# Backward SSD states: products and decays by head on ScalarE, the sum on VectorE

## The chip, the cores and the metric

The kernel runs on one core of a Trainium2 chip. The metric is the time of one execution on the device in microseconds; of several runs the median counts. A core has five engines, each with an instruction queue of its own: TensorE (PE, matmuls; PEld its weight loads), VectorE (DVE), ScalarE (ACT), GpSimd (POOL) and SyncE (SP), whose queue issues nearly all of this kernel's DMAs. Tiles lie in SBUF; matmuls write to PSUM.

## The reference, cut to what matters

The program is a backbone block of two layers over 1280 tokens, 256 of context and 1024 latent ones. Each layer projects the tokens, mixes them with two recurrences (an SSD group and an S5 group, both in both directions), and ends in a gated feed-forward net. The SSD scan works in chunks of 128 tokens; this is the part that the change touches, called once per direction:

```python
cum = jnp.cumsum(dt * a.reshape(SSD_GROUPS, SSD_HPG), axis=2)
xdt = xh * dt[..., None]
to_end = jnp.exp(cum[:, :, -1:] - cum)
states = jnp.einsum('bcqgn,bcqgep->bcgepn', bm, xdt * to_end[..., None])
chunk_decay = jnp.exp(cum[:, :, -1])

def step(h, inp):
    s, d = inp
    return h * d[..., None, None] + s, h
```

So a chunk gives a state from its values `xh`, weighted per token and head, and the running state is decayed by one number per head before the chunk's own is added. There are 8 heads of 64 channels; the running state of one direction is a tile of 128 by 512.

## The kernel before, in words

A layer goes through stages. After the projections for the S5 inputs comes a stretch in which VectorE runs the S5 scan: `s5_scan` makes one step after the other, four small tensor operations each (lines 545, 548, 549 and 550, tiles `sc` and `X`), and `s5_pairs` ends it with 96 operations on line 517. The whole scan is written into the program before the stage that follows.

In that stage `layer` (lines 1662 on) lets two things run together. `proj_z` makes the z projections: matmuls of 256 to 384 columns on lines 751 to 753 into four PSUM tiles `mm`, a ScalarE activation into `zb`, and a store. The generator `ssd_state` advances two steps with each piece of them and treats ten chunks in the order 1, 0, 9, 8, ..., 2. For a chunk it loads `xb` (six blocks of 128 by 128), transposes them on TensorE into two PSUM tiles, copies these to `xs` on ScalarE (lines 1196 and 1200), multiplies the values with `te` on GpSimd into `xe` (line 1168, in `ssd_xe`), and one step later stores `xs`, makes the state with two matmuls (`ssd_sum`) and hands it to `ssd_chain`. For the backward direction (`d` is 1, tile `hhb`) `ssd_chain` copies the state from PSUM to `hs` (line 1222, ScalarE), decays the running state (line 1223, GpSimd) and adds the two (line 1224, GpSimd). The first backward state is a plain copy (line 1219). Chunk 2 needs no backward state, so there are nine products and eight decays and sums in each layer. The forward direction (`hhf`), which also goes through `ssd_chain`, runs in the next stage, decayed on GpSimd and added on VectorE (lines 1226 and 1227).

The PSUM tiles `ps` of the transposes, the states and some small work share four buffers; in layer 0 the product of the conditioning weights (`adaw`) holds one of them for long. `xe` and `hs` share three buffers with the tag `yt`.

When all z projections are made and `ssd_state` is at its end, `s5_save` writes the scan's result to DRAM, eight stores `xh<-X`. SP's queue then goes on with loads for the next stage, among them `bto`, `xso` (values of a chunk), `cumrow` (decays) and later `xh`. Within a queue the order is fixed when the program is built: a scheduler places the instructions, and the helper class `Queue` only adds an order between a few of them. An instruction of a queue waits until those ahead of it have been issued.

Of the kernel before, what the change touches and what calls it, by code (L numbers as in the profile page):

```python
# [9 lines left out]
F32 = mybir.dt.float32  # L10
F32R = mybir.dt.float32r
I32 = mybir.dt.int32
AF = mybir.ActivationFunctionType
OP = mybir.AluOpType
AX = mybir.AxisListType

P = 128
# [81 lines left out]
class Kern:  # L99
# [1079 lines left out]
    def ssd_state(self, cs, S, xbc, dr, pool):  # L1179

        nc = self.nc
        XB, XT, XE = {}, {}, {}
        hb = None
        for t in range(len(cs) + 3):
            if t < len(cs):
                c = cs[t]
                XB[t] = pool.tile([P, 6, P], F32, name="xb", bufs=2)
                self.sp.dma_start(XB[t], xbc[4:10, :, c * P:(c + 1) * P].rearrange("m p t -> p m t"))
            t -= 1
            if 0 <= t < len(cs):  # L1190
                c, xb = cs[t], XB.pop(t)
                xt = XT[t] = pool.tile([P, 768], F32, name="xs", bufs=3)
                ps = self.psum()
                for i in range(4):
                    self.pe.transpose(ps[:, i * P:(i + 1) * P], xb[:, i], self.ident)
                nc.scalar.copy(xt[:, :512], ps)
                ps = self.psum()
                for i in range(2):
                    self.pe.transpose(ps[:, i * P:(i + 1) * P], xb[:, 4 + i], self.ident)
                nc.scalar.copy(xt[:, 512:], ps[:, :2 * P])  # L1200
                if c != 2:
                    XE[t] = self.ssd_xe(xt[:, :512], c, 1, S, pool)
            t -= 1
            if 0 <= t < len(cs):
                c, xt = cs[t], XT.pop(t)
                self.sp.dma_start(dr["xt"][c], xt)
                if c != 2:
                    hb = self.ssd_chain(self.ssd_sum(xt[:, 512:], XE.pop(t)), hb, c, 1, S, pool, "hb")
                    self.defer(1, lambda c=c, hb=hb: self.sp.dma_start(dr["hb"][c], hb))
            yield  # L1210

    def ssd_chain(self, cur, prev, c, d, S, pool, tag):

        nc, v, g = self.nc, self.nc.vector, self.nc.gpsimd
        h = pool.tile([P, 512], F32, name="h" + tag, tag=tag, bufs=2 if d else 3)
        v8 = lambda a: a.rearrange("p (h e) -> p h e", h=8)
        et = S["etot"][:, c, d].unsqueeze(2).to_broadcast([P, 8, 64])
        if prev is None:
            nc.scalar.copy(h, cur)
        elif d:  # L1220
            t = pool.tile([P, 512], F32, name="hs", tag="yt", bufs=self.ytb)
            nc.scalar.copy(t, cur)
            g.tensor_tensor(v8(h), v8(prev), et, op=OP.mult)
            g.tensor_tensor(h, h, t, op=OP.add)
        else:
            g.tensor_tensor(v8(h), v8(prev), et, op=OP.mult)
            v.tensor_tensor(h, cur, h, op=OP.add)
        return h
# [890 lines left out]
```

## Time and profile before

| what | value |
|---|---|
| median of three runs | 3443.62 us (3442.58 to 3463.33) |
| profiled execution | 3467.04 us, its span 3465.3 us |
| busy TensorE, VectorE, ScalarE, GpSimd | 3088.8, 2060.4, 1454.7, 1104.2 us |
| GpSimd product `xe` of the backward states | 9 per layer, 1.04 us each |
| GpSimd decay and sum | 8 per layer, 1.04 and 1.28 us each |
| the stage in layer 0, in layer 1 | from 434.4 us and from 2264.0 us of the span |

Positions are microseconds from the span's start. A line like L1224 is line 1224 of the kernel; L55 stands for the helper that records TensorE's and SP's instructions, so there the names of the tiles tell the place. In a name pair the tile before the arrow is written and those behind it are read. The busy time of an engine says nothing of its worth for the end; for that one has to see what waits where.

### The profile page before, as it was taken

Reading aid. Unit: us, or ns where it says so; the run is one execution under the profiler, and the core shown is the slowest. Engines: PE = TensorE matmul, PEld = TensorE weight load, DVE = VectorE, ACT = ScalarE, POOL = GpSimd, SP = SyncE. Lnnn points to the kernel's source line nnn. Section 1 sums busy time; section 2 is a strip of 40 time slices with the busy share of each in tenths; the row PEclk is TensorE's granted clock in tenths of the full one; section 3 lists DMA queues with packets and bytes.
Section 4 is the critical chain, followed back from the end, with each engine's and each line's share of the span. In section 5 each row is a group of like instructions: output and inputs, shape, how many; then the busy total and the mean of one; then the engine's idle time right before and its main releaser. Section 6 shows DMA issues by size and latency. Waiting matters only on the chain. (4 is left out here: it accounts for less than half of the span.)

```text
span 3465.3 us, 48617 instructions
## 1 busy us (share of the span) xinstructions
PE 3088.8 (89%) x18067; PEld 2673.7 (77%) x18067; DVE 2060.4 (59%) x3789; ACT 1454.7 (42%) x2610; POOL 1104.2 (32%) x847
## 2 busy tenths in 40 slices
PE   7689796898899999899999879775898999999998
PEld 4578674678879999889999769774576777877876
DVE  4875982456644444653344887993556655566555
ACT  4324522544543434543334443522545544454443
POOL 3651451213312323322222341451233333233230
PEclk8899897889999999999999889886889999999999
DMA  7345378525472222663322426268524533354332
GB/s 234 114 139 178 116 239 212 169 76 159 145 223 77 69 78 75 205 209 115 111 92 75 134 87 202 67 215 193 147 84 145 176 115 93 100 161 121 93 96 72
DMA packets 587281, 468.80 MB, mean 135 GB/s; under 512 B 59076, under 2 KB 506190, under 8 KB 587045
## 3 DMA queue, kind: packets, MB, share of 16 engines
q1 hardware_dynamic: 586565, 465.53, 44.5%
q8 instruction: 142, 2.33, 0.3%
q14 instruction: 94, 0.77, 0.1%
q0 software_dynamic: 480, 0.17, 0.0%
HBM read 355.99 MB, written 109.61 MB: 134 GB/s over the span
## 5 line engine op out<-in xcount | busy, mean ns | idle before, releaser
L860 POOL TENSOR_TENSOR ws<-rw,ws 128x512 fp32r<-128x512 f32 x352 | 483.9, 1377 | 1033.4 <-ACT ws L859 764.0
L752 PE MATMUL mm<-unit,ws 128*128 128x320 f32 (+3 forms) x2112 | 714.8, 338 | 3.4 <-POOL unit L901 3.4
L751 PE MATMUL mm<-unit,ws 128*128 128x320 f32 (+3 forms) x2112 | 716.5, 339 | 0.2 <-ACT unit L900 0.2
L753 PE MATMUL mm<-unit,ws 128*128 128x320 f32 (+3 forms) x2112 | 713.5, 338 | 0.0
L1439 DVE SCALAR_TENSOR_TENSOR fc<-fr,fcols,fc 128x255 f32<-128x255 f32 (+2 forms) x220 | 207.3, 958 | 492.7 <-ACT fc L1432 492.7
L751 PE MATMUL mm<-unit,whi 128*128 128x320 f32 (+3 forms) x1264 | 429.1, 341 | 38.0 <-ACT unit L900 23.4
L753 PE MATMUL mm<-unit,wlo 128*128 128x320 f32 (+3 forms) x1264 | 421.1, 334 | 31.4 <-POOL ub L996 19.0
L751 PEld LDWEIGHTS mm<-unit,ws 128*128 128x128 f32 x2112 | 398.0, 188 | 46.6 <-issue 10.1
L752 PEld LDWEIGHTS mm<-unit,ws 128*128 128x128 f32 x2112 | 398.0, 188 | 36.1 <-POOL unit L901 4.6
L753 PEld LDWEIGHTS mm<-unit,ws 128*128 128x128 f32 x2112 | 397.9, 188 | 34.7 <-issue 3.4
L752 PE MATMUL mm<-unit,whi 128*128 128x320 f32 (+3 forms) x1264 | 421.8, 334 | 2.6 <-POOL unit L901 1.6
L742 POOL TENSOR_TENSOR wlo<-raw,whi 128x1024 fp32r<-128x1024 f32 (+1 forms) x86 | 230.6, 2682 | 361.9 <-ACT whi L741 328.2
L751 PEld LDWEIGHTS mm<-unit,whi 128*128 128x128 f32 x1264 | 253.0, 201 | 74.7 <-ACT unit L900 25.4
L859 ACT CAST ws<-rw 128x512 fp32r<-128x512 f32 x352 | 218.4, 621 | 206.0 <-PE mm L753 116.8
L753 PEld LDWEIGHTS mm<-unit,wlo 128*128 128x128 f32 x1264 | 253.6, 201 | 47.3 <-POOL ub L996 19.2
L1519 DVE TENSOR_TENSOR acc<-mm,acc 128x256 f32<-128x256 f32 (+2 forms) x336 | 185.0, 554 | 171.2 <-PE mm L753 170.3
L752 PEld LDWEIGHTS mm<-unit,whi 128*128 128x128 f32 x1264 | 254.1, 201 | 15.3 <-issue 6.0
L751 PE MATMUL mm<-g,wd 128*128 128x320 f32 (+3 forms) x708 | 243.7, 345 | 10.8 <-ACT wd L859 6.8
L753 PE MATMUL mm<-g,wd 128*128 128x320 f32 (+3 forms) x708 | 241.5, 343 | 6.5 <-DVE wd L860 6.3
L752 PE MATMUL mm<-g,wd 128*128 128x320 f32 (+3 forms) x708 | 242.0, 342 | 0.0
L895 ACT COPY fr<-mm 128x320 f32<-128x320 f32 (+3 forms) x264 | 125.2, 476 | 195.1 <-PE mm L753 194.8
L1441 DVE SCALAR_TENSOR_TENSOR fc<-fr,fcols,fc 128x255 f32<-128x255 f32 (+2 forms) x220 | 176.0, 815 | 3.5
(390 smaller groups left out, 5761.5 us busy)
## 6 DMA issues: line engine op xcount, KB each, us to landing
rw<-in_ffn_w_up_dram SPq DMA_DIRECT2D x352, 256.0 KB
adaw<-in_w_ada_dram SPq DMA_DIRECT2D x80, 512.0 KB
raw<-in_ffn_w_down_dram SPq DMA_DIRECT2D x96, 384.0 KB
raw<-in_w_in_dram SPq DMA_DIRECT2D x40, 512.0 KB
raw<-in_w_out_dram SPq DMA_DIRECT2D x32, 512.0 KB
unit<-in_w_ada_dram SPq DMA_DIRECT2D x32, 256.0 KB
wt<-ws SPq DMA_DIRECT2D x32, 256.0 KB
ct<-w SPq DMA_DIRECT2D x64, 128.0 KB
```

The lines of the kernel that those rows point to most:

```text
L742: (eng or nc.vector).tensor_tensor(lo[:, :m], raw[:, :m], hi[:, :m].bitcast(F32), op=OP.subtract)
L751: mm(ps, whi[:, k], ahi[:, sl], start=first and k == 0, stop=False)
L752: mm(ps, whi[:, k], alo[:, sl], start=False, stop=False)
L753: i = mm(ps, wlo[:, k], ahi[:, sl], start=False, stop=last and k == len(a) - 1)
L859: self.nc.scalar.copy(hi, x)
L860: eng.tensor_tensor(lo, x, hi.bitcast(F32), op=OP.subtract)
L895: self.nc.scalar.copy(t[:, o:o + c], x)
L1439: v.scalar_tensor_tensor(cr[:, :, 1:], rr[:, :, :w - 1], f[0][:, ft:ft + 1], cr[:, :, 1:], op0=OP.mult, op1=OP.add)
L1441: v.scalar_tensor_tensor(cr[:, :, :w - 1], rr[:, :, 1:], f[2][:, ft:ft + 1], cr[:, :, :w - 1], op0=OP.mult, op1=OP.add)
L1519: v.tensor_tensor(acc[m][:, o:o + c], ps, acc[m][:, o:o + c], op=OP.add)
```

## The change

In `ssd_state` the product with `te` is made on ScalarE straight from the PSUM tile of the transposes, one activation per head of 128 by 64. In `ssd_chain` the backward decay is made on ScalarE too, again eight activations with a scale of one number per partition, and the state is added by one VectorE operation that reads it from PSUM; the copy to `hs` is gone, and GpSimd has no part in this stage's states. The forward direction is as it was.

```diff
@@ ssd_state
-                ps = self.psum()
+                px = self.psum()
                 for i in range(4):
-                    self.pe.transpose(ps[:, i * P:(i + 1) * P], xb[:, i], self.ident)
-                nc.scalar.copy(xt[:, :512], ps)
+                    self.pe.transpose(px[:, i * P:(i + 1) * P], xb[:, i], self.ident)
+                nc.scalar.copy(xt[:, :512], px)
...
                 if c != 2:
-                    XE[t] = self.ssd_xe(xt[:, :512], c, 1, S, pool)
+                    XE[t] = xe = pool.tile([P, 8, 64], F32, name="xe", tag="yt", bufs=self.ytb)
+                    for h in range(8):
+                        nc.scalar.activation(xe[:, h], px[:, h * 64:(h + 1) * 64], AF.Copy, scale=S["te"][:, c, 1, h:h + 1])
@@ ssd_chain
         elif d:
-            t = pool.tile([P, 512], F32, name="hs", tag="yt", bufs=self.ytb)
-            nc.scalar.copy(t, cur)
-            g.tensor_tensor(v8(h), v8(prev), et, op=OP.mult)
-            g.tensor_tensor(h, h, t, op=OP.add)
+            for i in range(8):
+                nc.scalar.activation(v8(h)[:, i], v8(prev)[:, i], AF.Copy, scale=S["etot"][:, c, d, i:i + 1])
+            v.tensor_tensor(h, cur, h, op=OP.add)
```

The change also moves instructions in the queues. On VectorE, at the end of layer 0's scan, before:

```order
L517 SCALAR_TENSOR_TENSOR X<-X,lam 128x2x81 x4
L517 SCALAR_TENSOR_TENSOR X<-X,lam 128x81 x8
L1264 MEMSET half 128x384
L1266 CAST half<-cumcol_5074 20x64 x2
L1312 TENSOR_TENSOR M<-M,E 128x512
```

and now, at the same place (line numbers behind the edit are one higher):

```order
L517 SCALAR_TENSOR_TENSOR X<-X,lam 128x2x81 x4
L517 SCALAR_TENSOR_TENSOR X<-X,lam 128x81 x8
L1225 TENSOR_TENSOR hhb<-ps,hhb 128x512 x8
L1265 MEMSET half 128x384
L1267 CAST half<-cumcol_5177 20x64 x2
```

All eight sums stand behind the scan's last operation; in layer 1 it is the same.

On TensorE, a chunk in the middle of layer 0's stage, with what it waits for (a name in the brackets is the engine or DMA ring whose work must be done), before:

```order
L753 MATMUL mm<-unit,wlo 128x320
L55 MATMUL ps<-ident,xb 128x128 [waits DMAHW4_49,Activation_49]
L55 MATMUL ps<-ident,xb 128x128 x3
L55 MATMUL ps<-ident,xb 128x128 [waits Activation_49]
L55 MATMUL ps<-ident,xb 128x128
L55 MATMUL ps<-xe,xs 128x256 [waits Activation_49,Pool_49]
L55 MATMUL ps<-xe,xs 128x256
```

and now, at the sixth of the ten chunks:

```order
L753 MATMUL mm<-unit,wlo 128x320
L55 MATMUL ps<-ident,xb 128x128 [waits DMAHW4_49,DVE_49]
L55 MATMUL ps<-ident,xb 128x128 x3
L751 MATMUL mm<-unit,whi 128x320
L752 MATMUL mm<-unit,whi 128x320
L753 MATMUL mm<-unit,wlo 128x320
```

The transpose, which waited for ScalarE to have read the PSUM buffer, now waits for VectorE, and z matmuls stand behind it.

On SP in the same stage, the first stores of the backward states that need a sum, before:

```order
L55 DMA hb_1021<-hhb 128x512 [waits DMAHW0_49,Pool_49]
L55 DMA xbc_1019<-zb 128x320 [waits DMAHW1_49,Activation_49]
L55 DMA xb<-xbc_1019 128x6x128 [waits DMAHW2_49,PE_49]
L55 DMA xt_1020<-xs 128x768 [waits DMAHW3_49]
L55 DMA xb<-xbc_1019 128x6x128 [waits DMAHW4_49,PE_49]
```

and now:

```order
L55 DMA hb_1021<-hhb 128x512 [waits DMAHW1_49,DVE_49]
L55 DMA hb_1021<-hhb 128x512 [waits DVE_49]
L55 DMA xb<-xbc_1019 128x6x128 [waits DMAHW3_49,PE_49]
L55 DMA xt_1020<-xs 128x768 [waits DMAHW4_49,Activation_49]
L55 DMA hb_1021<-hhb 128x512 [waits DMAHW5_49,DVE_49]
```

Stores that waited for GpSimd wait for VectorE, and loads of `xb` for later chunks stand behind them; the eight stores `xh<-X` follow the last of them, as before.

## Rows read from the trace of the kernel before

**Rows 1.** Windows: stretch, length, busy us of PE, PEld, DVE, ACT, POOL; PE clock; DMA share, GB/s.

```profile
434.40:517.50 83.10, 76.29 (x446) 64.80 (x447) 68.53 (x182) 21.49 (x45) 43.85 (x29) 0.94 0.71 235
2264.00:2323.80 59.80, 55.24 (x331) 52.56 (x331) 57.53 (x137) 19.85 (x41) 33.93 (x28) 0.95 0.70 231
553.20:563.20 10.00, 10.00 (x21) 5.67 (x22) 2.76 (x4) 2.98 (x5) 0.00 (x0) 0.50 0.48 160
```

**Rows 2.** Timeline, TensorE behind the stage: start, us, operation, [idle before <- released by].

```profile
553.20 1.19 PE L55 MATMUL ps<-cumrow,half 20*128 20x512 f32 x2 [33.21 <-DMA cumrow<-cum]
...
2374.65 2.04 PE L55 MATMUL ps<-xe,bto 128*128 128x256 f32 x4 [40.96 <-DMA bto<-xt]
```

**Rows 3.** Timeline, SP's queue: the stores of the scan and the load behind them.

```profile
518.99 21.78 SPq L55 DMA_DIRECT2D xh<-X  x8
...
2337.67 28.06 SPq L55 DMA_DIRECT2D xh<-X  x8
2365.83 3.22 SPq L55 DMA_DIRECT2D bto<-xt  x2
```

**Rows 4.** Timeline, VectorE and one row of GpSimd: scan steps and the scan's ends.

```profile
434.71 0.27 DVE L545 TENSOR_TENSOR sc<-X,lam 128x64 f32<-128x64 f32 x1
...
435.70 0.27 DVE L545 TENSOR_TENSOR sc<-X,lam 128x64 f32<-128x64 f32 x1
...
478.58 25.46 DVE L517 SCALAR_TENSOR_TENSOR X<-X,lam 128x162 f32<-128x162 f32 x96
504.06 0.38 DVE L1264 MEMSET half<- 128x384 f32 x1
...
2322.18 27.93 DVE L517 SCALAR_TENSOR_TENSOR X<-X,lam 128x162 f32<-128x162 f32 x96
2350.02 0.69 DVE L1227 TENSOR_TENSOR hhf<-ps,hhf 128x512 f32<-128x512 f32 x1
...
2350.79 1.04 POOL L1226 TENSOR_TENSOR hhf<-hhf,etot 128x512 f32<-128x512 f32 x1 [15.73 <-DVE hhf L1227]
```

**Rows 5.** Groups by line from 435.7 us on, GpSimd and the scan's steps | busy, mean ns.

```profile
L1224 POOL TENSOR_TENSOR hhb<-hhb,hs 128x512 f32<-128x512 f32 x8 | 10.3, 1293 | 0.7 <-ACT hs L1222 0.2
L1168 POOL TENSOR_TENSOR xe<-xs,te 128x512 f32<-128x512 f32 x9 | 9.4, 1043 | 14.2 <-ACT xs L1196 12.7 <-PE ps L55 1.4
L1223 POOL TENSOR_TENSOR hhb<-hhb,etot 128x512 f32<-128x512 f32 x8 | 8.4, 1045 | 2.1 <-DMA hb<-hhb 1.7
L742 POOL TENSOR_TENSOR wlo<-raw,whi 128x1024 fp32r<-128x1024 f32 x2 | 4.8, 2394 | 2.5 <-ACT whi L741 2.5
...
L545 DVE TENSOR_TENSOR sc<-X,lam 128x64 f32<-128x64 f32 x20 | 12.6, 632 | 0.7
```

**Rows 6.** Groups by line over the span, ScalarE and VectorE | busy us, mean ns | idle.

```profile
L1196 ACT COPY xs<-ps 128x512 f32<-128x512 f32 x20 | 11.7, 586 | 21.3 <-PE ps L55 21.3
L1200 ACT COPY xs<-ps 128x256 f32<-128x256 f32 x20 | 7.7, 384 | 0.0
L1049 ACT ACTIVATE cvp<-cvr,cols 128x320 f32<-128x320 f32 x24 | 12.0, 547 | 0.0
...
L1227 DVE TENSOR_TENSOR hhf<-ps,hhf 128x512 f32<-128x512 f32 x16 | 11.0, 689 | 35.1 <-PE ps L55 35.1
```

**Rows 7.** Timeline, ScalarE and TensorE in layer 0: prices of the small pieces.

```profile
426.19 1.00 ACT L1049 ACTIVATE cvp<-cvr,cols 128x320 f32<-128x320 f32 x2
...
466.17 1.03 PE L55 MATMUL ps<-xe,xs 128*128 128x256 f32 x4
467.77 0.82 PE L55 MATMUL ps<-ident,xb 128*128 128x128 f32 x6
...
471.02 0.31 PE L752 MATMUL mm<-unit,whi 128*128 128x320 f32 x1
471.17 0.31 PE L753 MATMUL mm<-unit,wlo 128*128 128x320 f32 x1
...
472.72 1.05 PE L55 MATMUL ps<-adaw,cv 128*32 128x512 f32 x4
```

## The prediction

> **What bounds the kernel now.** I read the slices of the page first, then two windows around the edited code, then who waits at their ends, then the queues. Each layer has a stage in which TensorE makes the z projections and, among them, the backward states of the SSD; VectorE meanwhile runs the S5 scan. VectorE is busy for 68.5 of 83.1 us of this stage in layer 0 and 57.5 of 59.8 us in layer 1, TensorE for 76.3 and 55.2 us [rows 1]. These windows end with the last z matmul, at 517.5 and 2323.8. Behind it TensorE stands still for 33.2 us in layer 0 and 41.0 us in layer 1, both times for a load [rows 2]. Those loads stand on SP's queue behind the eight stores of the scan's result, `xh<-X`, which start at 518.99 and 2337.67 and last 21.8 and 28.1 us [rows 3]. So what moves the start of these stores moves the kernel. In layer 0 the scan is done at 504.06, so the z projections, which end at 517.5, and the store of the last `zb` let the stores go. In layer 1 the scan ends only at 2350.0, after the z projections (2323.8), and half of the stores wait for it [rows 4].
>
> **What leaves GpSimd.** Per layer 9 products `xe` (9.4 us), 8 decays (8.4) and 8 sums (10.3): 28.1 of GpSimd's 32.9 us beside the scan [rows 5]. The scan feels them. A step of four instructions takes 0.99 us (434.71 to 435.70); the 20 steps from 435.70 to 478.58 take 42.9 us and not 19.8, so 23.1 us are lost to 32.9 us of GpSimd, 0.70 per us [rows 4, 5]. Taking 28.1 us away gives back 19.7 us. Layer 1 issues the same 25 instructions, and I take the same gain. The scan's end T moves from 504.1 to 484.4 and from 2350.0 to 2330.3. Bounds: 0 if something else stretches the steps, 28.1 if every us of GpSimd counts.
>
> **What the sums on VectorE do.** The eight new sums stand in VectorE's queue behind the last scan instruction, not among the scan's; the order of instructions shows it in both layers. The rows of before that show what such a place means are those of a forward sum in layer 1, which also stands behind the scan: it ran at 2350.02, at once behind the scan's 27.9 us, and GpSimd, whose next decay needs it, had by then waited 15.7 us [rows 4]. The Trainium skill, "Trace Analysis", section "Tensor Engine Instruction (MATMUL, LD_WEIGHTS)", states that VectorE, ScalarE and GpSimd work strictly in queue order. The trace agrees in the forward sum; if a waiting sum could pass the scan, the outcome would be the third rival below.
>
> So no sum runs before T. A sum holds its PSUM tile until it has run, and PSUM for these tiles has four buffers (one taken by the ada product in layer 0). With three held in layer 0 and four in layer 1, TensorE meets a transpose that waits for VectorE, and the z matmuls queue behind it. In the changed order 43.3 us of TensorE's work stand behind that transpose in layer 0: 30 transposes (0.82 us per six, 4.1), five pairs of sums (1.03 a pair, 5.2), four ada pairs (1.05, 4.2), 204 z matmuls (0.147 us apart at 320 columns, and in proportion at 256 and 384, 29.8) [rows 7]. In layer 1 it is 20.4 us: 24 transposes (3.3), four pairs (4.1), 84 z matmuls (13.0). TensorE reaches the transpose after some 30 to 40 us of its stage, that is near 470 and 2304, and idles until T.
>
> **The tail behind T.** Each remaining chunk costs ScalarE two copies (0.59 and 0.38 us), eight small activations for `xe` and eight for the decay. A pair of `cvp` activations with a scale from SBUF took 1.00 us at 320 columns, one 0.55, so 0.45 from start to start; 256 columns less at 0.79 ns each (from the two copies) leaves 0.25, and eight cost 2.0 us [rows 6, 7]. Above, 0.55 each without overlap and with no gain by width gives 4.4; below, 0.8 for eight at 0.10. I take 2.0, since the overlap is in the row. A link of the chain of states is decay 2.0, sum 0.69 [rows 6] and the hand-over, 2.85 us; eight links are 23 us, which is the least the tail can take.
>
> Layer 0: ScalarE has seven decays (14.0), four `xe` (8.0), five pairs of copies (4.9) and 1.5 us of others, 28.4 us; TensorE's work lies beside it, with a slow start: behind its 33 us of standing still TensorE works for 10 us at a granted clock of 0.50, the lower level, 1.2 GHz, before it rises [rows 1]. The last sum of states leaves TensorE near T+29, then 17.6 us of z matmuls and one 2 us of ada follow: the z projections end at T+50 = 534.4, 17 us later than 517.5. Today's waits of TensorE for loads in this stage are not in the sum, since the loads stand elsewhere on SP now; a few us for them stay in the range. The eight stores and the loads behind them then take what they take now: **+17 us**.
>
> Layer 1: ScalarE has seven decays, three `xe`, four pairs of copies, two `zb`: 24.8 us; the first sum and waits for TensorE's restart add some 11 us, the last sum is at T+36, the last `zb` behind two casts of weights at T+38 = 2368.3. SP stores `hb` and `zb` before the scan's result. All data then being ready, I take layer 0's 21.8 us for the stores: 2390.1. From there to TensorE it is 8.8 us now (2365.83 to 2374.65 [rows 2, 3]). Four us more are due, since the loads of the first two chunks, issued early now, stand behind the stores in the changed order, and their two states with them: 2403 against 2374.65, **+28 us**.
>
> The rest of the edit lies beside this: 25 GpSimd instructions fewer, 8 copies `hs` (0.59 each) fewer and 136 activations more per layer on a ScalarE that is busy 21.5 of 83.1 us here [rows 1]. Before T they are hidden by the scan; without that cover they would cost ScalarE's time of a chunk, 5 us.
>
> Sum: +45 us. The profiled execution took 3467.0 us, 23 us above the median of the runs, 3443.6. Against it the change gives 3512; against the median, which I forecast, **3489**.
>
> **Rivals.**
> - *The tail is as short as the chain of states* (23 us), TensorE's backlog fitting into it. Layer 1: 2330.3+23 = 2353, the stores end at 2375 (+9); layer 0: 507, before today's end of the z projections (0). +9 us, 3453. For it: ScalarE is idle most of the time. Against: 43.3 us of TensorE's work stand behind T in layer 0, 20 of it behind the last state.
> - *Much slower.* Activations at 0.55 each, a tail at the slow clock, loads `xb` behind the stores `hb` on SP: +20 us in each layer on top, 3529. Over the whole stage the granted clock is 0.94 [rows 1], which speaks against it.
> - *Faster.* The sums get in among the scan. Then TensorE does not stop, layer 1's stores end with a scan that is 19.7 us shorter, and layer 0 keeps its z projections: -20 us, 3424. It decides if VectorE takes a ready sum before the scan's end. For it: VectorE is the busiest engine of the stage and loses 23 us to GpSimd. Against: the place of the sums and the forward sum of layer 1. The Trainium skill, "Trace Analysis", section "Identifying the Most-Contended Engine", would have one relieve the engine of highest occupancy first; by that rule this rival would be the forecast.
>
> **Numbers.** Forecast 0.70, short tail 0.17, much slower 0.08, faster 0.05. The forecast's own range is 3465 to 3515 (15 us to either side in the two tails and the clock). The whole range, 3453 to 3525, reaches to the short tail and towards the slow one. One per cent is 34 us, about what a measurement here can tell from no change. Slower by more: three quarters of the forecast's 0.70 lie above 3478, plus the much slower case, 0.62; within: the rest of the forecast and the short tail, 0.33; faster 0.05.
>
> **What would show it.** The sums of L1225 start right behind the last L517, not before; TensorE idles some 15 us before 485 and 25 before 2330, ended by such a sum; the scan ends near 484 and 2330; the z projections end near 534, and `xh<-X` starts near 536 and 2368. Eight `xe` activations take 2 us. It is wrong if sums run among the scan's steps, if TensorE's stop is far shorter, or if the holes behind the stage shrink by as much as the stage grows.

## The result and the profile after

The changed kernel takes 3476.63 us (median of 17 runs) against 3451.89 us of the kernel before on the same chip: a ratio of 1.007, 95% interval 1.0054 to 1.0086, that is 19 to 30 us more. The sign and the mechanism were forecast; the size, +45 us, was nearly twice what came.

VectorE and one row of TensorE in layer 0 of the change (timeline: start, us, engine, line, operation, count, [idle before it <- released by]):

```profile
454.87 23.32 DVE L517 SCALAR_TENSOR_TENSOR X<-X,lam 128x162 f32<-128x162 f32 x96
478.09 0.70 DVE L1225 TENSOR_TENSOR hhb<-ps,hhb 128x512 f32<-128x512 f32 x1
480.88 0.69 DVE L1225 TENSOR_TENSOR hhb<-ps,hhb 128x512 f32<-128x512 f32 x1 [2.09 <-ACT hhb L1224]
...
478.85 1.12 PE L55 MATMUL ps<-ident,xb 128*128 128x128 f32 x4 [16.21 <-DVE hhb L1225]
```

The first sum runs at 478.09, at once behind the scan's last operation. TensorE has stood still for 16.21 us and goes on when that sum has read its PSUM tile. This is the wait that the change put in; nothing of the kind is in the trace of before. In layer 1 it is longer:

```profile
2289.99 23.32 DVE L517 SCALAR_TENSOR_TENSOR X<-X,lam 128x162 f32<-128x162 f32 x96
2313.21 0.70 DVE L1225 TENSOR_TENSOR hhb<-ps,hhb 128x512 f32<-128x512 f32 x1
2316.00 0.69 DVE L1225 TENSOR_TENSOR hhb<-ps,hhb 128x512 f32<-128x512 f32 x1 [2.09 <-ACT hhb L1224]
2318.80 0.69 DVE L1225 TENSOR_TENSOR hhb<-ps,hhb 128x512 f32<-128x512 f32 x1 [2.10 <-ACT hhb L1224]
2322.58 0.69 DVE L1225 TENSOR_TENSOR hhb<-ps,hhb 128x512 f32<-128x512 f32 x1 [3.09 <-ACT hhb L1224]
2327.73 0.69 DVE L1225 TENSOR_TENSOR hhb<-ps,hhb 128x512 f32<-128x512 f32 x1 [4.46 <-ACT hhb L1224]
2333.39 0.69 DVE L1225 TENSOR_TENSOR hhb<-ps,hhb 128x512 f32<-128x512 f32 x1 [4.97 <-ACT hhb L1224]
2336.39 0.69 DVE L1225 TENSOR_TENSOR hhb<-ps,hhb 128x512 f32<-128x512 f32 x1 [2.30 <-ACT hhb L1224]
2339.26 0.69 DVE L1225 TENSOR_TENSOR hhb<-ps,hhb 128x512 f32<-128x512 f32 x1 [2.18 <-ACT hhb L1224]
...
2313.97 1.11 PE L55 MATMUL ps<-ident,xb 128*128 128x128 f32 x4 [26.35 <-DVE hhb L1225]
```

These eight sums are one chain: each waits for ScalarE's decay of the running state, which waits for the sum ahead of it. Eight sums with their links take 26.7 us (2313.21 to 2339.95); the shortest link is 2.79 us, and the longer ones have ScalarE's other work in them. The scan's last 96 operations take 23.32 us in both layers, against 25.46 and 27.93 [rows 4], and nearly all of its steps take 0.98 us; three beside a split `wlo` on GpSimd, one in layer 0 and two in layer 1, take 3.1 to 3.2.

Then SP's stores of the scan's result and TensorE behind them, in both layers (the rows that answer to [rows 2, 3]):

```profile
526.32 21.68 SPq L55 DMA_DIRECT2D xh<-X  x8
...
2341.92 22.08 SPq L55 DMA_DIRECT2D xh<-X  x8
2364.10 2.88 SPq L55 DMA_DIRECT2D bto<-xt  x1
...
559.72 1.19 PE L55 MATMUL ps<-cumrow,half 20*128 20x512 f32 x2 [31.87 <-DMA cumrow<-cum]
...
2374.59 3.78 PE L55 MATMUL ps<-xe,bto 128*128 128x256 f32 x8 [32.84 <-POOL xe L1168]
...
2373.50 3.21 POOL L1168 TENSOR_TENSOR xe<-xso,te 128x512 f32<-128x512 f32 x3 [23.92 <-DMA xso<-xt]
```

TensorE's hole behind the stage is nearly as long as before in layer 0 and 8 us shorter in layer 1, since there the stores now go out at one stretch. Its releaser in layer 1 is GpSimd's `xe`, which had itself waited 23.92 us for the load of `xso`; so it is still a load behind those stores.

Positions of two profiles can't be compared as they stand. The two first profiles, before and after, both have a span of 3465.3 us, though the medians differ by 25 us: between the two stages the kernel before took 1710.9 us (553.20 to 2264.07), the changed one 1692.4 (559.72 to 2252.09), with the same number of matmuls (10452). So I measure a stage from its first transpose of `xb` to the first matmul behind the hole, and the scan's end from that same transpose. This is done for all kernels of the next section as well, with one profile each. "Both against before" is the sum of the two stages less its mean over the two profiles of before; "in us" is the ratio's share of 3452 us:

| kernel | scan's end, layer 0, 1 | stage, layer 0, 1 | both against before | ratio, interval | in us |
|---|---|---|---|---|---|
| before, first profile | 69.6, 86.0 | 118.8, 110.6 | | | |
| before, second (e1) | 70.5, 86.8 | 110.8, 112.0 | | | |
| change, first profile | 46.2, 61.2 | 127.7, 122.5 | +24.1 | 1.007, 1.0054 to 1.0086 | +24 |
| change, second (e8) | 46.5, 59.9 | 128.5, 118.7 | +21.1 | | |
| e2 sum on GpSimd | 54.5, 72.1 | 123.8, 96.7 | -5.5 | 0.9988, 0.997 to 1.0006 | -4 |
| e3 sum alone on VectorE | 51.0, 65.9 | 133.7, 120.9 | +28.5 | 1.0121, 1.0095 to 1.0146 | +42 |
| e4 sums among last groups | 60.7, 71.0 | 118.7, 109.7 | +2.4 | 1.0028, 1.0006 to 1.005 | +10 |
| e5 sums among the steps | 61.8, 80.0 | 109.5, 99.4 | -17.1 | 0.9964, 0.9948 to 0.9979 | -12 |
| e6 and early stores | 61.3, 79.8 | 92.2, 104.0 | -29.8 | 0.9944, 0.992 to 0.9968 | -19 |
| e7 product alone | 65.1, 79.6 | 114.2, 104.2 | -7.7 | 0.9983, 0.9967 to 1.0 | -6 |

On the mean of two profiles each the two stages are 22.6 us longer, against 24 by the runs. The rest of the program varied from 3214 to 3239 us over these ten profiles, as much as the effect itself, and no run explains it (in the change's two profiles it was 13 us shorter than in those of before). So the column of the runs says which kernel is faster, and the stages only say where. In e5 and e6 the first matmul behind layer 1's hole is another one, which waits for the load of `xh` and not of `bto`.

### The profile page after: what moved, and what is told of

It is laid out like the page before. It is cut to its first block, busy times and chain, and to the rows that moved or that the text cites. A ratio compares the mean times of both kernels' runs of the same rounds, so it can differ in the third digit from the quotient of the medians.

```text
span 3465.3 us, 48811 instructions
## 1 busy us (share of the span) xinstructions
PE 3081.2 (89%) x18067; PEld 2671.9 (77%) x18067; DVE 2031.9 (59%) x3805; ACT 1501.9 (43%) x2864; POOL 1006.8 (29%) x797
## 4 chain that ended last, share of the span: by engine, by line
PE 41%; DVE 12%; DMA 3%; ACT 3%; issue 2%; SPq 1%; POOL 1%; DVEq 0%; ACTq 0%; POOLq 0%
PE mm L751 12%; PE mm L753 12%; PE mm L752 12%; PE ps L55 5%; SPq L55 1%; DVE X L550 1%; DVE fc L1440 1%; DVE fc L1442 1%; DMA xs<-md 1%; DVE X L517 1%; DVE sc L545 1%; DVE X L549 1%; DVE sc L548 1%; DVE t L256 1%; DVE w L255 1%
## 5 line engine op out<-in xcount | busy, mean ns | idle before, releaser
L751 PE MATMUL mm<-unit,whi 128*128 128x320 f32 (+3 forms) x1264 | 427.4, 340 | 42.2 <-ACT unit L900 25.9
L742 POOL TENSOR_TENSOR wlo<-raw,whi 128x1024 fp32r<-128x1024 f32 (+1 forms) x86 | 195.5, 2274 | 532.9 <-ACT whi L741 490.9
```

What stands on the lines that cost most here:

```text
L742: (eng or nc.vector).tensor_tensor(lo[:, :m], raw[:, :m], hi[:, :m].bitcast(F32), op=OP.subtract)
L751: mm(ps, whi[:, k], ahi[:, sl], start=first and k == 0, stop=False)
```

## Experiments

The theory: the loss comes from the place of the sums in VectorE's queue, behind the scan, since a sum that waits holds PSUM and that stops TensorE. The rivals: ScalarE's 136 more activations a layer cost the time (72 for the products, 64 for the decays), or the stages vary by as much from run to run.

**e1, the kernel before once more, and e8, the change once more.** No edit.

> The kernel before, unchanged, for a second profile. Its first profile took 3467.0 us, 15 us above the median of its 17 runs, 3451.9, and that of the changed kernel 3467.1, 10 us below its median, 3476.6. If the change is worth what the medians say (+25 us), a profile of the kernel before near its median shows the two stages as in the first profile: from the stage's first transpose to the load's end that lets TensorE go on, about 119 us in layer 0 and 111 us in layer 1, against 127.7 and 122.5 us in the changed kernel (together +21), and the rest of the program shorter by some 15 us than in the first profile. The rival, that the stages themselves vary by as much as the change, would show other than 119 and 111 us here by more than 5 us.

It took 3457.5 us. Layer 1's stage was 112.0 us, as expected; layer 0's was 110.8 and not 119, and the rest of the program 3 us shorter than in the first profile, not 15. So here the rival was partly right: layer 0's stage varies. Both profiles show one cause. GpSimd in layer 0, first in the first profile of before, then in the second:

```profile
495.13 10.06 POOL L742 TENSOR_TENSOR wlo<-raw,whi 128x512 fp32r<-128x512 f32 x1 [14.25 <-ACT whi L741]
```

```profile
495.50 1.45 POOL L742 TENSOR_TENSOR wlo<-raw,whi 128x512 fp32r<-128x512 f32 x1 [13.41 <-ACT whi L741]
```

The same instruction, which splits weights for the next stage, takes 10.06 or 1.45 us beside VectorE's stream of L517. SP's next load `raw` goes out at 505.22 or 496.97, and with it the loads `adaw` and stores `zb` behind it; in the first profile TensorE then waits 3.95 us for `adaw`, in the second it doesn't. That covers about half of the 8 us; TensorE also worked at a mean granted clock of 0.94 in the first and 0.98 in the second up to the stores.

> The change as it is, for a second profile, since two profiles of the kernel before differ by 8 us in layer 0's stage (119 and 111 us from the stage's first transpose to TensorE's going on behind the loads) and by 1.4 us in layer 1's (110.6 and 112.0). The first profile of the change has 127.7 and 122.5 us. If these are its own, and not a disturbed execution's, the second has 125 to 130 and 120 to 125 us, a stop of TensorE ended by the first sum of 16 and 26 us, within 2, and the scan's end 46 and 61 us behind the first transpose, within 2. If layer 0's stage varies here as it does before the change, it has 120 us or less there.

The second profile of the change has 128.5 us in layer 0, and stops of 16.4 and 25.4 us; layer 1 has 118.7, 1.3 under the expected 120. The change's times are its own, within 4 us.

**e2, the sum back on GpSimd** (against the change).

```diff
+            t = pool.tile([P, 512], F32, name="hs", tag="yt", bufs=self.ytb)
+            nc.scalar.copy(t, cur)
             for i in range(8):
                 nc.scalar.activation(v8(h)[:, i], v8(prev)[:, i], AF.Copy, scale=S["etot"][:, c, d, i:i + 1])
-            v.tensor_tensor(h, cur, h, op=OP.add)
+            g.tensor_tensor(h, h, t, op=OP.add)
```

> The change with one part undone: the sum of states stays on GpSimd, behind a ScalarE copy of the state, as before; products and decays are on ScalarE as in the change. Theory (the loss comes from the sums' place behind the scan on VectorE): no stop of TensorE ended by a sum; the scan, with 17.8 us of GpSimd less beside it, ends 12 to 15 us earlier in each layer than before; layer 0 keeps the end of its z projections (83 us behind the stage's first transpose, within 4), and in layer 1 the stores of the scan's result are done some 8 us earlier: 3444 us, ratio 0.9975 (0.994 to 1.001). Rival (the loss is ScalarE's, 136 activations more per layer): ScalarE still has all of them and the copies as well, so ratio 1.006 or more, with the z projections of layer 0 ending 8 us or more later than before.

Ratio 0.9988: all of the loss is gone with the place of one operation (and the copy that feeds it), while ScalarE has every activation of the change and eight copies more. That excludes the rival's 1.006. The scan ends 15.5 and 14.3 us earlier than in before's two profiles on their mean (70.0, 86.4; expected 12 to 15). The gain in layer 1 is larger than expected (14.5 us), and layer 0 loses: its stores start 90.7 us behind the first transpose, not 83. TensorE has one stop of 11.26 us there, ended by ScalarE's `zb`; ScalarE had waited, and behind that stood GpSimd (timeline of e2, ScalarE, GpSimd, TensorE):

```profile
471.81 12.71 POOL L1227 TENSOR_TENSOR hhb<-hhb,hs 128x512 f32<-128x512 f32 x1 [0.58 <-ACT hhb L1226]
...
484.55 2.02 ACT L1226 ACTIVATE hhb<-hhb,etot 128x64 f32<-128x64 f32 x8 [10.00 <-POOL hhb L1227]
486.47 0.47 ACT L1030 ACTIVATE zb<-mm 128x384 f32<-128x384 f32 x1
...
486.99 0.69 PE L751 MATMUL mm<-unit,whi 128*128 128x384 f32 x1 [11.26 <-ACT zb L1030]
```

One sum, which takes 1.28 us elsewhere, took 12.71 until the stream of L517 was over (483.4). The decay behind it waits, `zb` waits behind the decay, and TensorE waits for `zb`'s PSUM tile. So a decay on ScalarE is a new way for a late sum to stop TensorE. Layer 0's stage came out 9.0 us longer than before, against the 14.5 us that layer 1 won.

**e3, the sum alone on VectorE**, products and decays on GpSimd as before (against the kernel before).

```diff
-            t = pool.tile([P, 512], F32, name="hs", tag="yt", bufs=self.ytb)
-            nc.scalar.copy(t, cur)
             g.tensor_tensor(v8(h), v8(prev), et, op=OP.mult)
-            g.tensor_tensor(h, h, t, op=OP.add)
+            v.tensor_tensor(h, cur, h, op=OP.add)
```

> The kernel before with one part of the change alone: the sum of states on VectorE straight from PSUM, no copy by ScalarE; products and decays stay on GpSimd. Theory (place of the sums): TensorE stops as in the change, and for longer, since only 10.3 us of GpSimd leave the scan: the scan ends about 8 us earlier than before (61 and 78 us behind the stage's first transpose, against 46 and 61 in the change), TensorE stands still from 30 to 36 us until then, and what is queued behind takes as long as in the change or a little less (decay 1.04 us on GpSimd against 2.0): 45 us in layer 0, 25 in layer 1, so +20 and +20 us: 3492 us, ratio 1.012 (1.007 to 1.018), above the whole change's 1.007. Rival (ScalarE's small activations are the loss): without them the ratio is at most 1.002.

Ratio 1.0121, the expected 1.012, and slower than the whole change. TensorE's waits in layer 0 and in layer 1 of e3 (who waited <- for whom: us in total, times, the longest):

```profile
PE ps L55 <- DVE hhb L1222: 22.0, 3, 20.3
```

```profile
PE ps L55 <- DVE hhb L1222: 29.4, 3, 21.8
```

So the sum alone brings the loss, with no activation added. Two numbers missed: the scan ended at 51.0 and 65.9 us, not at 61 and 78, since GpSimd, whose decays wait for the sums, also stands still while the scan runs; and the stages account for 28.5 of 42 us; where the rest is, one profile doesn't tell (the stretch between the stages varied by 18 us in the first four profiles).

**e4, the sums among the scan's last groups.** The scan's remaining 11 steps and eight groups of L517 are written into the stage; `sums` holds the sums written so far, `npairs` counts the groups, and each group is ordered behind the sum of its number (against the change; the lines that fill the two are left out):

```diff
             self.flush()
-            go(200)
...
                 for _ in self.proj_z(l, H, m, W(), pz, xbc, py):
-                    pass
+                    if self.npairs < 0:
+                        go(11)
+                        self.npairs = 0
+                    while self.npairs < len(self.sums):
+                        go(1)
...
+                if post and self.npairs < len(self.sums):
+                    self.order(it, self.sums[self.npairs])
```

> The whole change, with the scan's last eight groups of 12 operations (L517) written into the program beside the states, each behind one sum, so that VectorE's queue alternates: sum, 12 operations, sum, and so on. Nothing else differs. Theory (place of the sums): TensorE's stops ended by a sum shrink from 16 and 26 us to under 6; the scan ends 5.5 to 10 us later than in the change (about 53 and 69 us behind the stage's first transpose), the z projections of layer 0 end as before (83 us, within 4), and in layer 1 the stores are done 8 us earlier than before: 3442 us, ratio 0.997 (0.993 to 1.001), some 34 us better than the change. Rival (ScalarE's activations, or PSUM and SP's new order, hold the stage whatever the sums' place): ratio 1.004 or more.

Ratio 1.0028: better than the change, but a miss, since it lies above the theory's range and below the rival's. Sums and groups alternate as meant, yet TensorE stopped for 9.7 and 18.3 us and not under 6, ended by the first sum both times:

```profile
453.97 2.08 PE L55 MATMUL ps<-xe,xs 128*128 128x256 f32 x4 [9.66 <-DVE hhb L1227]
```

```profile
2288.78 1.54 PE L55 MATMUL ps<-ident,xb 128*128 128x128 f32 x6 [18.27 <-DVE hhb L1227]
```

The stop begins 14 us behind the stage's first transpose, not 31 to 36 as in the change, since TensorE's queue moved too: 38 and 34 z matmuls stand between the first transpose and the stop, against 117 and 151 in the change; the first sum, behind the steps, came at 23 and 32 us. Either the theory was right and the sums still too late, or something else holds the stage at this level. e5 tells these apart.

**e5, the sums among the steps as well.** 23 steps (layer 0) and 39 (layer 1) are held back and written into the chain. `self.scan` (`s`) counts the pieces written and the sums, and lists how many pieces stand ahead of each sum; a piece is a step or a group of L517 (against the change; the lines in `s5_pairs` and `s5_scan` that order each piece behind the sum ahead of it are left out):

```diff
-                    go(10)
+                    go(3 if last else 7)
             self.flush()
-            go(200)
+            self.scan = [0, 0, None, [10, 14, 19, 24, 29, 34, 38, 40] if last else [8, 12, 16, 20, 24, 25, 26, 27], scan, None]
...
+            s = self.scan
+            while s[0] < s[3][s[1]]:
+                next(s[4])
+                s[0] += 1
-            v.tensor_tensor(h, cur, h, op=OP.add)
+            it = v.tensor_tensor(h, cur, h, op=OP.add)
+            if s[5] is not None:
+                self.order(it, s[5])
+            s[1], s[2] = s[1] + 1, it
```

> The whole change, with 23 (layer 0) and 39 (layer 1) steps of the scan and its eight last groups written into the program beside the states, so that VectorE's queue has the first sum behind 8 (10) steps and the others 4 or 5 steps, or one group, apart; nothing else differs. In the run with the sums among the last groups alone TensorE still stopped for 9.7 and 18.3 us, from 14 us behind the stage's first transpose, until the first sum, at 23 and 32 us. Theory (a sum's place in VectorE's queue sets how long it holds PSUM, and that stops TensorE): stops ended by a sum are under 3 us each; the scan ends 53 and 68 us behind the first transpose; layer 0's z projections end at 77 to 84 us as before, layer 1's stores are done about 90 us behind it instead of 102: TensorE goes on 111 to 119 and 100 us behind the first transpose: -10 us against before, 3442 us, ratio 0.997 (0.993 to 1.000). Rival (ScalarE, now 5 us per chunk with the small activations, holds the z projections' PSUM): stops of TensorE ended by ScalarE take the place of the sums', ratio 1.002 or more.

Ratio 0.9964 (0.9948 to 0.9979), expected 0.997: the whole change, with nothing but the place of the scan's instructions in the program altered, is faster than the kernel before. By the stages most of it lies in layer 1 (99.4 us against 110.6 and 112.0); in layer 0 the 109.5 stand against 118.8 and 110.8. Whether writing the scan later would help the kernel before as well was not tried, so the -12 us are not shown to be the worth of the change alone. TensorE's stops ended by a sum, layer 0 and the longest of layer 1:

```profile
468.96 0.87 PE L55 MATMUL ps<-ident,xb 128*128 128x128 f32 x6 [0.63 <-DVE hhb L1237]
478.10 1.13 PE L55 MATMUL ps<-xe,xs 128*128 128x256 f32 x4 [0.37 <-DVE hhb L1237]
...
2272.89 1.11 PE L55 MATMUL ps<-ident,xb 128*128 128x128 f32 x4 [2.92 <-DVE hhb L1237]
```

All are under 3 us, and stops ended by ScalarE did not take their place (the longest, 1.4 us in layer 1, is for a cast of weights). The stages are 109.5 and 99.4 us (expected 111 to 119 and 100). The scan itself ends later than I expected, 61.8 and 80.0 us; VectorE waits for the first sum's decay, 6.0 us in layer 0 and 9.00 us in layer 1, so that sum stands somewhat too early. In layer 0 the scan still ends 14.5 us before its stores start; in layer 1 two stores go out at 67 us and the other six from 78 us, when the scan is nearly done.

**e6, in layer 0 the scan's stores among the z projections' stores** (against e5).

```diff
                 for _ in self.proj_z(l, H, m, W(), pz, xbc, py):
-                    pass
+                    if not last and self.scan[1] == 8:
+                        go(200)
+                        next(save, None)
```

`save` gives one of the eight stores `xh<-X` at a time, each ordered behind the one before it, in layer 1 too.

> The kernel with the sums among the steps, and in layer 0 the eight stores of the scan's result placed one by one among the last z projections' stores on SP, not behind them all; layer 1 as there. Theory (what stands behind the scan's stores on SP is what TensorE waits for, so their end sets it): the scan ends 30 us before the z projections there, so the stores are out when these end, TensorE's hole of 32 us behind layer 0's stage falls to some 12, and the time to 20 us below the kernel with the sums among the steps: 3422 us, ratio 0.991 (0.987 to 0.996). Rival (the same transfers are only moved: their 16 engines are then busy while zb stores and weights need them, and TensorE waits among the z projections instead): no gain against the other, ratio 0.996 or more.

Ratio 0.9944 (0.992 to 0.9968): inside the theory's range, but short of its 0.991, and the interval reaches over 0.996, where the rival begins. In the trace it does what the theory says: the eight stores lie between 478.38 and 511.0, and layer 0's stage falls from 109.5 to 92.2 us. What is late next are two shorter waits of TensorE in place of the one of 32 us:

```profile
514.65 1.92 PE L55 MATMUL ps<-adaw,cv 128*32 128x512 f32 x4 [7.22 <-DMA adaw<-in_w_ada_dram]
523.48 2.07 PE L55 MATMUL ps<-xe,bto 128*128 128x256 f32 x4 [6.91 <-POOL xe L1177]
```

By the runs the gain over e5 is 2 thousandths, 7 us, and the two intervals overlap. The stages agree with that once both are measured to the same matmul, the first `ps<-cumrow,half`: layer 0 falls from 109.5 to 94.3 us, but layer 1 rises from 101.5 to 109.2, 7.6 us less in all. In layer 1 the scan's stores end 5 us later than in e5, with one of them ahead of the wait for the scan and not two; whether the new order among them does that, or chance, is open. Both e5 and e6 beat the kernel before and the change.

**e7, the product alone on ScalarE**, decay, copy and sum as before (the first part of the change's diff, nothing of the second).

> The kernel before with the first part of the change alone: the products xe on ScalarE from PSUM; the decay, the copy and the sum as before. 9.4 us of GpSimd leave the scan, ScalarE has 72 small activations more per layer (0.25 us each). Theory: the scan ends 6 to 9 us earlier in each layer; layer 0, bound by the z projections, keeps its time, layer 1's stores end 4 to 8 us earlier: 3446 us, ratio 0.998 (0.995 to 1.001). Rival (small activations of ScalarE cost the kernel time): ratio 1.003 or more, with waits of TensorE for ScalarE in the z projections.

Ratio 0.9983 (0.9967 to 1.0), expected 0.998; the scan ends 5 and 6.8 us earlier than the mean of before (expected 6 to 9); the stages are 114.2 and 104.2 us. TensorE waits nowhere in them for ScalarE. So the small activations of the products cost nothing, and relieving the scan of GpSimd seems to gain a little where nothing is queued behind it: the interval just reaches 1.0, so the gain is not clear of noise.

## Why the prediction was right, and where its sizes failed

- **The place of the sums decides: right, and shown.** The rows at 478.09 and 2313.21 are what it named, e3 has the loss from this operation alone, e2 loses the loss with it, and e5 turns the sign by order alone. The third rival's condition, the sums among the scan, is what e5 makes: by the runs it gives -12 us where the rival said -20. VectorE is the busiest engine only in layer 1's stage (57.5 us, TensorE 55.2); in layer 0's it is TensorE, 76.3 against 68.5 [rows 1]. The Trainium skill, "Perfetto Trace Analysis", section "Identifying the Most-Contended Engine", would relieve the engine of highest occupancy first; e5, whose gain lies mostly in layer 1, agrees, and in the change the relief was taken back by the wait.
- **The scan's end: right in sign, too small.** Forecast 19.7 us earlier; on the mean of two profiles each it is 23.7 and 25.9. The factor 0.70 came from the steps alone [rows 4, 5]. On the mean the last 96 operations are 2.7 and 4.6 us shorter (23.32 and not 25.46 to 27.93), since other GpSimd work that lay beside them (`wlo`, the forward `xe`) now falls elsewhere; that I had not counted. The steps gained the other 21 us, 0.75 per us of the 28.1 taken off GpSimd.
- **TensorE's stops: right.** About 15 and 25 us forecast, 16.2 and 26.4 measured, though behind the first transpose they begin some 5 us, and end 3 to 4 us, earlier than I had it.
- **Small activations: right.** Eight decays take 2.02 us (478.83) and eight products 1.80 (487.93), forecast 2.0; the lower bound of 0.10 us each had no row behind it:

```profile
478.83 2.02 ACT L1224 ACTIVATE hhb<-hhb,etot 128x64 f32<-128x64 f32 x8 [18.61 <-DVE hhb L1225]
...
487.93 1.80 ACT L1204 ACTIVATE xe<-ps,te 128x64 f32<-128x64 f32 x8
```

- **Layer 0's tail: nearly right.** The z projections' end was forecast at T+50 and the stores near T+52; the stores start 48.1 us behind the scan's end (478.2 to 526.3) and last 21.7 us. The forecast's +17 was counted from the first profile of before, and against that one the stage is 9.3 us longer on the mean of the change's two: the scan's end and the tail came some 4 us early each. Against the second profile, where `wlo` did not take 10.06 us, it is 17.3 us longer; that this equals the forecast is luck.
- **Layer 1's tail: the term that failed.** I put the last `zb` at T+38: 24.8 us of ScalarE, and 11 us for the first sum and TensorE's restart, added to it. The last `zb` was out at T+28 (2341.36, its store). The 24.8 us held: ScalarE is busy for 24.1 of the 27.6 us from the scan's end to its last `zb`. The 11 us did not come: the first sum and all of ScalarE's waits are 3.5 us, since TensorE's work lies beside ScalarE's and hardly holds it up. The restart was also milder: in the 10 us behind the stops the granted clock was 0.81 and 0.75 on the mean, a mix of its two levels, and not the 0.50 that I took over from [rows 1]. Windows of the change (stretch, length, busy PE, PEld, DVE, ACT, POOL, PE clock, DMA share, GB/s):

```profile
2313.31:2340.91 27.60, 23.82 (x130) 21.64 (x130) 5.83 (x10) 24.08 (x94) 0.78 (x1) 0.87 0.76 253
478.85:488.85 10.00, 10.00 (x58) 8.88 (x59) 2.08 (x3) 9.81 (x41) 0.00 (x0) 0.81 0.46 161
2313.97:2323.97 10.00, 10.00 (x49) 9.76 (x50) 2.08 (x3) 8.78 (x35) 0.00 (x0) 0.75 0.48 159
```

  SP's queue behind the last `zb`, in layer 1:

```profile
2341.36 0.51 SPq L55 DMA_DIRECT2D xbc<-zb  x1
2341.92 22.08 SPq L55 DMA_DIRECT2D xh<-X  x8
```

  From the stores' start to TensorE it is 32.7 us (forecast 34.6). The first profile of the change has layer 1's stage at 122.5 us where the sum had 139 (2403 less 2264): the scan's earlier end is 5 us of the 16.5 (61.2 against 66.3), the tail 9.4, the stores and loads 1.9. On the means of two profiles the two layers give +13.3 and +9.3 where the forecast had +17 and +28.
- **Chances.** 3476.63 us lies in the forecast's own range (3465 to 3515), but a change of 0.7% is under the 1% for which I gave 0.62 (the terms given there make 0.605). It is told from no change all the same: the interval is 0.5% to 0.9%. Part of the nearness to 3489 is luck, since the median of before came out at 3451.89 and not at the 3443.62 that I started from; 25 us on top of that would have been 3468, near the range's foot. The range was right to reach far down; the tail's separate waits should not have been added where they could overlap.

## What to carry to other kernels

Before an operation is moved to another engine, look up where it comes to stand in that engine's queue, and what it holds while it waits there: here 0.69 us of VectorE, eight times, made the change 24 us slower than the kernel before, though the scan had gained as much, since the states that waited for them held PSUM tiles until the scan was over. If the work it is queued behind can be split, write the two in alternation; the same work then gave -12 us in place of +24. And take a second profile of the kernel before where a stage's length carries the argument.

## What the runs showed of the hardware

GpSimd beside a close stream of VectorE operations with operands in SBUF can be held for long or not at all: the split `wlo` took 10.06 or 1.45 us, the sum in e2 12.71 instead of 1.28, and both long ones ended 1.1 us behind the last L517 (504.04 and 483.40). The others beside such a stream took 1.1 to 3.5 us. The Trainium skill, "SBUF — State Buffer", section "SBUF: two separate sides", calls the port pair that the two engines share an exclusive lock, held by whichever instruction started first, while the other blocks. The steps of the scan agree with that: operations of 0.27 us [rows 4] became 0.63 on the mean of L545 beside GpSimd's of 1.04 to 1.3 us [rows 5], and are 0.27 us again in the change, where GpSimd is nearly idle beside them. For the long ones such a lock would have to pass GpSimd by for dozens of VectorE instructions; what lets one in and not another was not tried.
